# Turning the normalised mixer outputs of three heads in float32r, from copies, behind the next head's softmax

## The chip, the cores and the metric

The kernel runs as one program on one core of a Trainium2 chip. The metric is its device time in microseconds (us). The kernel before takes 1347.12 us, the median of three runs (1346.63 to 1347.56).

## What is computed

The reference is a two-layer backbone over 256 latent tokens and 256 context tokens of 1024 features. Layer 0 has an mLSTM mixer, layer 1 multi-head latent attention, and a gated ConvFFN follows each. Everything is float32. The change lies in the mLSTM mixer of layer 0. It has four heads with 512 value features each, and its output is:

```python
def out(h_in, s):
    Bq, T, _ = h_in.shape
    o = jax.nn.sigmoid(h_in @ w_og).reshape(Bq, T, M_HEADS, M_DV)
    hsum = o * s.transpose(0, 2, 1, 3).astype(h_in.dtype)
    return _head_rms_norm(hsum, norm_g) @ w_out
```

Here `s` is the result of the scan, which the kernel computes for a head as one masked, weighted product P v over all 512 tokens. So a head's tokens are multiplied by a gate, divided by their root mean square over the head's 512 features, scaled by a gain for each feature, and then multiplied by `w_out`, whose contraction runs over the features.

## The kernel before

**Products in three passes.** A float32 product is made of float32r products: every operand is kept as a float32r tile that holds its rounded value and a second one that holds the rest, and `mm3` (L425 to L434) issues first times first, first times second, second times first. Weights come from HBM in tiles of 128 x 1024, are rounded on ScalarE (L345) and their rest is formed on VectorE (L368). A transpose is a product with an identity matrix; `post` uses the float32 identity `ident`.

**A mixer head.** `w_qk(h)` makes the head's q and k from the convolved input: eight weight tiles with 24 matmuls each. `s_mm(h)` forms the scores S. `head(h, S)` is the softmax-like part: it loads two rows of gate values (`aB`, L1045), adds masks (`Am`), takes exponentials (`W`, L1087), multiplies them with S, normalises the rows to P and turns P on TensorE (L1118). `v_load(h)` loads the head's values `vr` and gates `oh`. `av(h)` multiplies P with v and the result with the gate (L1178); the four tiles of 128 tokens x 512 features that it gives are `tt`.

**What the change touches.** `post(h, tt)` takes them: four Squares with sums (L1188), a square root (L1189), a reciprocal, four scalings in place (L1192), then a `yield`; then sixteen transposes of 128 x 128 (L1198) in four groups, each group written out with the gain as a pair of float32r tiles `hn` (L1205 on ScalarE, L1206 on VectorE). `outmm("mout", ...)` multiplies `hn[k]` with `w_out`, for k from 0 to 15, with four k for each head; 12 matmuls a k.

**What sets the order.** `head`, `post` and others are generators, kept in the list `k.bg`. `tick` advances the first of the list by one `yield`; a generator that has ended costs one tick to be taken off. `w_qk` ticks twice after each of its eight weight tiles, and the output projection twice after each k from 0 to 7 and once after each k from 8 to 15. A planner then orders each engine's instructions: it follows the order in which the program issues them, takes something later where an instruction's inputs or its buffer are not there by its own estimate, and each engine runs its list in the order that results. The list of POOL holds the DMAs that are issued there: `vr`, `oh`, `aB`, the residual and gate rows.

**Before the change**, `post(h - 2)` stands ahead of `head(h - 1)` in the loop over heads for h = 2 and 3: norm at tick 1, transposes at tick 2, taken off at tick 3, the softmax at ticks 4 to 8 and P turned at tick 9. In the output projection `head(3)` stands first (ticks 1 to 6) and `post(2)` after it (ticks 8 and 9). `post(3)` runs behind k = 8 and 9 of the projection.

**Buffers.** Tiles of 128 x 512 float32 come from a pool called "s2" with NS = 15 buffers: `tt` (that is `oh`), S, `aB`, `Am`, `W`, `vr`, Squares' output `jk`. A tile of the pool can be written only when one of the 15 is free.

Of the kernel before, what the change touches and what calls it, by code (L numbers as in the profile page):

```python
# [7 lines left out]
F32 = mybir.dt.float32  # L8
F32R = mybir.dt.float32r
I32 = mybir.dt.int32  # L10
AF = mybir.ActivationFunctionType
ALU = mybir.AluOpType
# [21 lines left out]
NB, NRAW, NU, NS = 3, 3, 31, 15  # L34
# [366 lines left out]
class K:  # L401
# [73 lines left out]
    def setup(self):  # L475
        nc, p = self.nc, self.pool
        a = self.a
        self.sm = p.tile([128, a["sm"].shape[1]], F32, name="sm")
        self.sm0 = p.tile([128, NSM0], F32, name="sm0")
        jp = p.tile([128, 128], I32, tag="s2", name="jp", bufs=NS)  # L480
        nc.gpsimd.iota(jp, pattern=[[1, 128]], base=0, channel_multiplier=-1)
        self.jp = jp
        self.ident = p.tile([128, 128], F32, name="ident")
        self.mask = p.tile([128, 2, 128], F32, name="mask")
        self.k1 = p.tile([128, 1], F32, name="k1")
        nc.vector.memset(self.k1, 1.0)
        self.zero = p.tile([128, 512], F32R, tag="s2", name="zero", bufs=NS)
        nc.vector.memset(self.zero.bitcast(F32), 0.0)
        self.keps = p.tile([128, 1], F32, name="keps")
        nc.vector.memset(self.keps, EPS)  # L490
        self.cond = p.tile([128, 8, 32], F32, tag="s2", name="cond", bufs=NS)
        nc.gpsimd.memset(self.cond, 0.0)
        self.mod0 = p.tile([128, 2, 8, 2], F32, name="mod0")
        self.modc = {(0, c): self.mod0[:, c] for c in range(2)}
        self.gd = {}
        self.adav = p.tile([128, 32], F32, name="adav")
        nc.vector.memset(self.adav, 0.0)
        for l in range(2):
            for c in (3, 4) if l == 0 else (0, 1, 3, 4):
                self.modc[l, c] = p.tile([128, 8, 2], F32, name="mod%d%d" % (l, c))  # L500
            for c in (2, 5):
                self.gd[l, c] = self.dr.tile([2, D], F32, name="gd%d%d" % (l, c))
# [102 lines left out]
    def start_up(self):  # L605
# [47 lines left out]
        with self.tc.manual_schedule(engines={e.PE, e.DVE, e.Activation}):  # L653
            for _ in range(WARM):
                nc.tensor.matmul(idle, self.zero[:, 0:128], self.zero, start=True, stop=True)
            for step in STEPS:
                op, n = step[0], [int(x) for x in step[1:]]
                g = n[0]
                if op == "Q":
                    nc.scalar.activation(self.cond[:, :, 0:2], self.smc("cond").rearrange("p (a b) -> p a b", b=2),  # L660
                                         AF.Silu)
                    nc.vector.tensor_scalar(self.ident, self.jp, 0.0, None, op0=ALU.is_equal)
                    b1 = self.smc("ada_b")[:, 8:16]
                    nc.vector.tensor_scalar(b1, b1, 1.0, None, op0=ALU.add)
                elif op == "M":
                    nc.vector.tensor_scalar(self.mask[:, 0], self.jp, 0.0, NEG, op0=ALU.is_gt, op1=ALU.mult)
                    nc.vector.tensor_scalar(self.mask[:, 1], self.jp, 0.0, NEG, op0=ALU.is_lt, op1=ALU.mult)
                    self.jp = None
                elif op == "I":
                    for _ in range(g):  # L670
                        nc.tensor.matmul(idle, self.zero[:, 0:128], self.zero, start=True, stop=True)
                elif op in "Aab":
                    if g not in rows:
                        rows[g] = self.ps("adar")
                    self.ada_mm(rows[g], [(x, raw["a%d%d" % (g, x)]) for x in {"A": (0, 1), "a": (0,), "b": (1,)}[op]])
                elif op == "C":
                    adas[g] = self.ada_copy(rows[g])
                elif op == "T":
                    self.ada_T(rows[g], adas[g])
                elif op == "O":  # L680
                    self.ada_cols(g, rows[g])
                elif op == "E":
                    self.mod_tile(g)
                elif op == "H":
                    h = hT[g] = self.u("hT")
                    self.split(h[:, 0, :], h[:, 1, :], self.xT[g])
                elif op == "e":
                    h = hT[g] = self.u("hT")
                    x, (c, l) = self.xT[g], (slice(0, 256), slice(256, 512))
                    sh, sc = self.modc[0, 0][:, g], self.modc[0, 1][:, g]  # L690
                    nc.vector.tensor_scalar(x[:, c], x[:, c], sc[:, 1:2], sh[:, 1:2], op0=ALU.mult, op1=ALU.add)
                    nc.scalar.activation(h[:, 0, l], x[:, l], AF.Identity, bias=sh[:, 0:1], scale=sc[:, 0:1])
                    nc.vector.tensor_copy(h[:, 0, c], x[:, c])
                elif op == "l":
                    nc.vector.tensor_scalar(x[:, l], x[:, l], sc[:, 0:1], sh[:, 0:1], op0=ALU.mult, op1=ALU.add)
                    nc.vector.tensor_sub(h[:, 1], x, h[:, 0])
                elif op in "WwvyzKkU":
                    if op == "U":
                        g = "u"
                        raw["wu"] = raw["u0"]  # L700
                    if g not in w:
                        w[g] = [self.pool.tile([128, CW], F32R, tag="u", name="w0", bufs=NU) for _ in range(2)]
                    c = slice(256, nw) if op in "yz" else slice(0, 256 if op in "wv" else 768 if op == "U" else nw if g < 2 else 512)
                    hi, lo, src = w[g][0][:, c], w[g][1][:, c], raw["w%s" % g][:, c]
                    if op == "w":
                        nc.vector.tensor_copy(hi, src)
                    elif op in "WyKU":
                        nc.scalar.copy(hi, src)
                    if op in "WvzkU":
                        nc.vector.tensor_sub(lo, src, hi)  # L710
                else:
                    k, m = n
                    if m not in ps:
                        ps[m] = self.ps("up")
                    wk, o = (w["u"], k - 2) if m == 4 and k > 1 else (w[k], m)
                    c = slice(o * 128, (o + 1) * 128)
                    for i, j in {"V": ((0, 0), (0, 1), (1, 0)), "P": ((0, 0),), "L": ((1, 0),), "R": ((0, 1),)}[op]:
                        nc.tensor.matmul(ps[m], wk[i][:, c], hT[k][:, j], start=made[m] == 0, stop=made[m] == 23)  # L718
                        made[m] += 1
# [460 lines left out]
        self.PT = self.vh = self.oh = None  # L1180
        return r

    def post(self, h, tt):
        nc = self.nc
        ss = self.tiny(4, "ss")
        jk = self.s2("jk")
        for t in range(4):
            nc.scalar.activation(jk, tt[t], AF.Square, accum_out=ss[:, t:t + 1])  # L1188
        nc.scalar.activation(ss, ss, AF.Sqrt, bias=self.keps, scale=1.0 / 512.0)  # L1189
        nc.vector.reciprocal(ss, ss)  # L1190
        for t in range(4):
            nc.vector.tensor_scalar(tt[t], tt[t], ss[:, t:t + 1], None, op0=ALU.mult)  # L1192
        yield
        g = self.smc("mng")
        for e in range(4):
            pt = self.ps("hnT")
            for t in (2, 0, 1, 3):
                q = nc.tensor.transpose(pt[:, t * 128:(t + 1) * 128], tt[t][:, e * 128:(e + 1) * 128], self.ident)  # L1198
                if e or t != 2:
                    self.behind(q, [lead])  # L1200
                else:
                    lead = q
            k = h * 4 + e
            u = self.u("hn")
            nc.scalar.activation(u[:, 0], pt, AF.Copy, scale=g[:, k:k + 1])  # L1205
            nc.vector.scalar_tensor_tensor(u[:, 1], pt, g[:, k:k + 1], u[:, 0], op0=ALU.mult, op1=ALU.subtract)  # L1206
            self.hn[k] = u
        yield


    def bcast(self, row, name):
        ts = []
# [969 lines left out]
def build(tc, off, a, out):  # L2182
    es = ExitStack()
    with es:
        k = K(tc, es, off, a)
        nc = k.nc
# [16 lines left out]
        for h in range(H0):  # L2203
# [1 line left out]
            if h == 0:  # L2205
                gens.append(k.gate_chain())
            if h >= 2:
                gens.append(k.post(h - 2, tt))
            if h >= 1:
                gens.append(k.head(h - 1, S))  # L2210
            k.bg = gens
            k.w_qk(h, 2, (lambda: k.v_load(h - 1)) if h >= 1 else None)
# [4 lines left out]
        k.xc = None  # L2217
        hn = lambda i: (k.hn[i][:, 0], k.hn[i][:, 1])
        pc = k.acc4()
        k.bg = [k.head(3, S, True), k.post(2, tt)]  # L2220
        vs = k.v_steps(3)
        for i in range(8):
            k.outmm("mout", range(i, i + 1), hn, pc, 0, 16, 2, n2=ADA_M)
            next(vs, None)
        k.drain()
        tt = k.av(3)
        k.bg = [k.post(3, tt)]
        k.outmm("mout", range(8, 12), hn, pc, 0, 16, 1, n2=ADA_M)
        k.drain()
        tokr = a["tok"].rearrange("(t p) d -> t p d", p=128)  # L2230
# [132 lines left out]
```

## Time and profile before

| What | Value |
|---|---|
| median of three runs | 1347.12 us |
| the profiled execution, span from first to last instruction | 1345.3 us, 1.8 us below the median |
| TensorE (PE) busy | 1334.9 us |
| weight loads of TensorE (PEld) busy | 1120.2 us |
| VectorE (DVE), ScalarE (ACT), GpSimd (POOL) busy | 1059.0, 711.7, 141.5 us |
| transposes of `post` | 64, in four batches of 16 that begin at 465.06, 524.25, 598.46 and 615.22 us |
| turning of P | four times 12; those after head 0 at 487.39, 546.57 and, in two parts, 584.96 and 594.80 us |

The span is what the profiler saw between the first and the last instruction. PEld runs beside PE, so the two are not added. A matmul's duration is longer than its share of the pipeline: matmuls start closer together than they last, and the distance between starts tells what one costs. In a row of the time line stand start, duration, engine, line, operation, written tile, read tiles, shape and count; in brackets stands the idle time of the engine before it and what ended it. In a row of groups the busy time and the mean duration in ns stand behind the bar. DMA-issuing rows of POOL show the issue; "us to landing" is the time until the data are there.

### The profile page before, as it was taken

Reading aid. Unit: us, or ns where it says so; the run is one execution under the profiler, and the core shown is the slowest. Engines: PE = TensorE matmul, PEld = TensorE weight load, DVE = VectorE, ACT = ScalarE, POOL = GpSimd, SP = SyncE. Lnnn points to the kernel's source line nnn. Section 1 sums busy time; section 2 is a strip of 40 time slices with the busy share of each in tenths; the row PEclk is TensorE's granted clock in tenths of the full one; section 3 lists DMA queues with packets and bytes.
Section 4 is the critical chain, followed back from the end, with each engine's and each line's share of the span. In section 5 each row is a group of like instructions: output and inputs, shape, how many; then the busy total and the mean of one; then the engine's idle time right before and its main releaser. Section 6 shows DMA issues by size and latency. Waiting matters only on the chain.

```text
span 1345.3 us, 18750 instructions
## 1 busy us (share of the span) xinstructions
PE 1334.9 (99%) x6659; PEld 1120.2 (83%) x6659; DVE 1059.0 (79%) x1745; ACT 711.7 (53%) x1252; POOL 141.5 (11%) x236
## 2 busy tenths in 40 slices
PE   9999999999999999999999999999999999999997
PEld 5777888888888888888898888888888998988886
DVE  4798656678688696897979977758899889898874
ACT  4765444445744546474644334333566767676660
POOL 0222000011101011020002011111000002000100
PEclk9999999999999999999999999999999999999999
DMA  9988848889686384776628989967866437376750
GB/s 364 330 277 279 281 163 248 233 272 307 235 281 230 102 255 149 228 292 222 215 86 261 328 260 286 282 181 184 300 223 194 157 104 219 127 212 189 263 189 32
DMA packets 99885, 304.02 MB, mean 226 GB/s; under 512 B 12312, under 2 KB 25112, under 8 KB 99712
## 3 DMA queue, kind: packets, MB, share of 16 engines
q1 hardware_dynamic: 62992, 218.65, 48.6%
q0 software_dynamic: 26000, 66.75, 17.9%
q10 hardware_dynamic: 10800, 17.44, 3.6%
q8 instruction: 52, 0.85, 0.3%
q14 instruction: 41, 0.34, 0.1%
HBM read 272.21 MB, written 42.12 MB: 234 GB/s over the span
## 4 chain that ended last, share of the span: by engine, by line
PE 97%; DMA 1%; DVE 1%; ACT 0%; issue 0%; SPq 0%; DVEq 0%; ACTq 0%
PE fin L1503 8%; PE tok L430 6%; PE tok L434 6%; PE tok L433 6%; PE fin L433 6%; PE fin L434 6%; PE y L433 6%; PE fin L430 6%; PE y L434 6%; PE y L430 6%; PE qk L430 4%; PE qk L433 4%; PE qk L434 4%; PE up L718 2%; PE up L430 2%; PE up L434 1%
## 5 line engine op out<-in xcount | busy, mean ns | idle before, releaser
L368 DVE TENSOR_TENSOR w<-raw,w 128x1024 fp32r<-128x1024 f32 (+2 forms) x286 | 343.2, 1203 | 131.9 <-ACT w L345 129.7
L345 ACT CAST w<-raw 128x1024 fp32r<-128x1024 f32 (+2 forms) x286 | 296.2, 1037 | 282.4 <-PE tok L434 77.8
L544 DVE SCALAR_TENSOR_TENSOR junk<-ar,bc 128x1024 f32<-128x1024 f32 x128 | 156.1, 1219 | 5.2 <-ACT bc L586 2.3
L433 PE MATMUL fin<-h,w 128*128 128x512 f32 (+1 forms) x370 | 139.6, 377 | 0.0
L430 PE MATMUL fin<-h,w 128*128 128x512 f32 (+1 forms) x370 | 139.5, 377 | 0.0
L434 PE MATMUL fin<-h,w 128*128 128x512 f32 (+1 forms) x370 | 139.3, 377 | 0.0
L1503 PE MATMUL fin<-h,w 128*128 128x512 f32 (+1 forms) x636 | 111.1, 337 | 0.0
L1503 PEld LDWEIGHTS fin<-h,w 128*128 128x128 f32 x636 | 97.6, 190 | 13.2
L430 PE MATMUL qk<-xc,w 128*128 128x512 f32 x256 | 100.2, 391 | 0.0
L434 PE MATMUL qk<-xc,w 128*128 128x512 f32 x256 | 99.8, 390 | 0.0
L433 PE MATMUL qk<-xc,w 128*128 128x512 f32 x256 | 99.6, 389 | 0.0
L433 PEld LDWEIGHTS fin<-h,w 128*128 128x128 f32 x370 | 69.6, 188 | 13.0
L430 PEld LDWEIGHTS fin<-h,w 128*128 128x128 f32 x370 | 69.6, 188 | 12.9
L434 PEld LDWEIGHTS fin<-h,w 128*128 128x128 f32 x370 | 69.6, 188 | 12.6
L434 PEld LDWEIGHTS qk<-xc,w 128*128 128x128 f32 x256 | 48.0, 188 | 10.1
L430 PEld LDWEIGHTS qk<-xc,w 128*128 128x128 f32 x256 | 48.1, 188 | 9.8
L433 PEld LDWEIGHTS qk<-xc,w 128*128 128x128 f32 x256 | 48.1, 188 | 9.8
L430 PE MATMUL tok<-w,hT 128*128 128x512 f32 x128 | 49.9, 390 | 0.0
L433 PE MATMUL tok<-w,hT 128*128 128x512 f32 x128 | 49.8, 389 | 0.0
L434 PE MATMUL tok<-w,hT 128*128 128x512 f32 x128 | 49.8, 389 | 0.0
L735 ACT ACTIVATE fg<-fg 128x512 f32<-128x512 f32 (+1 forms) x44 | 23.1, 525 | 50.0 <-DVE fg L733 43.9
L368 DVE TENSOR_TENSOR wu<-raw,wu 128x1024 fp32r<-128x1024 f32 (+1 forms) x37 | 43.8, 1203 | 3.5 <-ACT wu L345 3.2
(486 smaller groups left out, 3125.7 us busy)
## 6 DMA issues: line engine op xcount, KB each, us to landing
raw<-in_ws SPq DMA_DIRECT2D x282, 512.0 KB, 4.5
ar<-in_adaT SPq DMA_DIRECT2D x80, 512.0 KB, 6.0
t4d<-in_ws POOLq DMA_DIRECT2D x20, 512.0 KB, 9.1
adaw<-in_ada SPq DMA_DIRECT2D x16, 512.0 KB, 8.0
zr<-fd ACTq DMA_DIRECT2D x33, 128.0 KB, 4.6
xmd<-xr POOLq DMA_DIRECT2D x16, 256.0 KB, 4.4
xcd<-cv POOLq DMA_DIRECT2D x16, 256.0 KB, 4.9
xs<-xmd POOLq DMA_DIRECT2D x16, 256.0 KB, 6.0
```

Source lines behind the costliest of these rows:

```text
L345: self.cast = k.nc.scalar.copy(h[:, :cols], src)
L368: i = self.k.nc.vector.tensor_sub(l[:, :n], src, h[:, :n])
L430: q = mm(out, w[0], x[0], start=start, stop=False, skip_group_check=on)
L433: mm(out, w[0], x[1], start=False, stop=False, skip_group_check=on)
L434: mm(out, w[1], x[0], start=False, stop=stop, skip_group_check=on)
L544: nc.vector.scalar_tensor_tensor(o, w, 1.0, self.bc[j], op0=ALU.mult, op1=ALU.mult, accum_out=col[:, k, j:j + 1])
L718: nc.tensor.matmul(ps[m], wk[i][:, c], hT[k][:, j], start=made[m] == 0, stop=made[m] == 23)
L735: nc.scalar.activation(tmp[:, :n], tmp[:, :n], AF.Silu)
L1503: self.nc.tensor.matmul(ps[:, 0:256] if x else ps, w[x][:, k * 128:(k + 1) * 128], h[:, 0:256] if x else h, start=i == 0 and not k0, stop= ...
```

## The change

Three things change in the mixer of layer 0.

- For heads 0, 1 and 2, each scaled tile `tt[t]` is copied by a DMA on POOL's queue, word for word, into a tile `rr` of the type float32r from the pool "s2". The transposes read `rr` and a float32r identity `identr`, and write PSUM as float32r. For head 3 they read `tt` and the float32 identity as before.
- A new generator `around` issues the norm and the copies of `post` in its first tick, then all of the next head's `head`, and then the rest of `post`. In the loop over heads the softmax so comes at ticks 2 to 6, P is turned at tick 7 and the transposes of `post` are issued at tick 9. In the output projection the norm of head 2 moves ahead of `head(3)`.
- `post` has one `yield` more between norm and transposes. For head 3 the transposes so come behind k = 10 of the projection and not k = 9.

`identr` is written once, on VectorE, beside the masks at the end of the start-up.

```diff
+        self.identr = p.tile([128, 128], F32R, name="identr")
...
+                    nc.vector.tensor_scalar(self.identr, self.jp, 0.0, None, op0=ALU.is_equal)
...
-    def post(self, h, tt):
+    def post(self, h, tt, copy=True):
...
+        rr = []
         for t in range(4):
             nc.vector.tensor_scalar(tt[t], tt[t], ss[:, t:t + 1], None, op0=ALU.mult)
+            if copy:
+                r = self.pool.tile([128, 512], F32R, tag="s2", name="rr", bufs=NS)
+                nc.gpsimd.dma_start(r.bitcast(F32), tt[t])
+                rr.append(r)
+        src, ident, dt = (rr, self.identr, F32R) if copy else (tt, self.ident, F32)
+        yield
         yield
...
-                q = nc.tensor.transpose(pt[:, t * 128:(t + 1) * 128], tt[t][:, e * 128:(e + 1) * 128], self.ident)
+                q = nc.tensor.transpose(pt[:, t * 128:(t + 1) * 128].bitcast(dt), src[t][:, e * 128:(e + 1) * 128], ident)
...
+    def around(self, post, head):
+        next(post)
+        yield
+        yield from head
+        yield from post
...
             if h >= 2:
-                gens.append(k.post(h - 2, tt))
-            if h >= 1:
+                gens.append(k.around(k.post(h - 2, tt), k.head(h - 1, S)))
+            elif h >= 1:
                 gens.append(k.head(h - 1, S))
...
-        k.bg = [k.head(3, S, True), k.post(2, tt)]
+        k.bg = [k.around(k.post(2, tt), k.head(3, S, True))]
...
-        k.bg = [k.post(3, tt)]
+        k.bg = [k.post(3, tt, False)]
```

## The prediction

> **What bounds the kernel now.** I read the page first, then the groups of TensorE by shape, then the time lines around the places that the change touches.
>
> ```profile
> PE 1334.9 (99%) x6659; PEld 1120.2 (83%) x6659; DVE 1059.0 (79%) x1745; ACT 711.7 (53%) x1252; POOL 141.5 (11%) x236
> PE 97%; DMA 1%; DVE 1%; ACT 0%; issue 0%; SPq 0%; DVEq 0%; ACTq 0%
> ```
>
> TensorE (PE) is busy for 1334.9 of 1345.3 us, and 97% of the chain of waits is its own work. So a copy, a scale or a DMA is worth something only if PE waits for it, and a gain must come out of PE's own time. The change touches 48 transposes of PE, in three batches of 16. What a batch costs is read from the time line of PE around each (start, duration, count):
>
> ```profile
> 462.73 0.39 PE L434 MATMUL qk<-xc,w 128*128 128x512 f32 x1
> ...
> 464.77 0.39 PE L434 MATMUL qk<-xc,w 128*128 128x512 f32 x1
> 465.06 2.03 PE L1198 MATMUL hnT<-ident,oh 128*128 128x128 f32 x16
> 466.85 0.48 PE L430 MATMUL qk<-xc,w 128*128 128x512 f32 x1
> 467.17 0.40 PE L433 MATMUL qk<-xc,w 128*128 128x512 f32 x1
> ...
> 523.96 0.39 PE L434 MATMUL qk<-xc,w 128*128 128x512 f32 x1
> 524.25 2.03 PE L1198 MATMUL hnT<-ident,oh 128*128 128x128 f32 x16
> 526.04 0.48 PE L430 MATMUL qk<-xc,w 128*128 128x512 f32 x1
> 526.35 0.40 PE L433 MATMUL qk<-xc,w 128*128 128x512 f32 x1
> ...
> 598.23 0.39 PE L434 MATMUL y<-w,hn 128*128 128x512 f32 x1
> 598.46 1.91 PE L1198 MATMUL hnT<-ident,oh 128*128 128x128 f32 x16
> 600.12 0.47 PE L430 MATMUL y<-w,hn 128*128 128x512 f32 x1
> 600.44 0.39 PE L433 MATMUL y<-w,hn 128*128 128x512 f32 x1
> ```
>
> Nine undisturbed 512-column matmuls lie between 462.73 and 464.77: 0.227 us a step. From the last matmul before a batch to the second after it lie 2.40, 2.39 and 2.21 us; less two normal steps (0.45), the batches cost 1.94, 1.94 and 1.75 us, 5.63 in all. The third is undisturbed: 1.75 / 16 = 0.109 us per transpose. The first two hold about 0.18 more each, since their scaled inputs arrive while they run.
>
> **What a float32r transpose costs.** The trace has none, nor any float32r matmul under 256 columns; two things can limit it, the streaming of the moving identity and the load of the stationary block.
>
> ```profile
> L433 PE MATMUL qk<-xc,w 128*128 128x512 f32 x256 | 99.6, 389 | 0.0
> L1503 PE MATMUL fin<-h,w 128*128 128x256 f32 x320 | 44.6, 282 | 0.0
> L764 PE MATMUL gates<-cv,gw 128*32 128x512 f32 x32 | 3.8, 598 | 0.0
> L1198 PE MATMUL hnT<-ident,oh x64: 270/273/328, 465.1 to 616.9; 128*128 128x128 f32 x64
> L718 PE MATMUL up<-hT,w x120: 387/389/504, 10.1 to 48.0; 128*128 128x512 f32 x120
> 1149.72 2.32 PE L1346 MATMUL y<-wu,oT 128*128 128x256 f32 x18
> 1151.88 1.36 PE L1439 MATMUL fin<-h,wu 128*128 128x256 f32 x10
> ```
>
> Streaming: the first two rows are float32r tiles (every product of L430 to L434 and L1503 is). 256 columns more cost 107 ns, so 128 columns stream in 53.5. The gate matmuls (third row) read plain float32, and 512 columns take 209 ns longer than in float32r: one more pass. A float32r matmul of 128 columns would by this last 282 - 53.5 = 229; the present transposes last 273, 44 more, so they too run two passes, and 0.109 us is two times 53.5 and little else. In float32r I expect one.
>
> Load: a matmul that had to wait for its own load shows it in its duration. For the transposes the longest less the median is 328 - 273 = 55 ns, for float32r matmuls (L718) 504 - 389 = 115. Which holds for a float32r transpose, no row says. If what is loaded is decided by the transpose, 55 hides behind the stream; if by the type, 115 is the step.
>
> So the step p has these ends: 55 from below (load and stream overlapped, nothing on top), 120 from above (what 18 float32r matmuls of 256 columns take each, 2.16 / 18). I take 62: one pass of 53.5 plus some of the 13 ns that a 512-column step of 227 has beyond its 214 of streaming. It is the nearer value because plain float32 in the same transpose already loads in 55.
>
> A rule of the Trainium skill speaks against it. "TensorE: Matmul & The Clock Gate", section "LDWEIGHTS (loading the stationary operand)", puts a load at its number of columns divided by 1.2, in ns, whatever the rows: an estimate by that page of 107 for these blocks, and then nothing is gained. The 115 of L718 agrees with it, the 55 of the present transposes does not, so here the rule holds for one kind of load and is open for the new one.
>
> **The change, part by part.**
>
> Transposes: a batch now costs 15 p, and its last one hides only a part of the 115 ns load of the float32r matmul behind it: 15 x 0.062 + 0.115 = 1.05 us. The inputs will long be there, so the 0.18 of the first two batches goes too. Saved: 0.89 + 0.89 + 0.70 = 2.5 us. With p = 55: 0.94 a batch, 2.8 saved. With p = 120: 1.92 a batch, 0.02 + 0.02 - 0.17, or 0.1 lost.
>
> Copies: twelve DMAs of 256 KB on POOL's queue, four behind each normalisation.
>
> ```profile
> oh<-od POOLq DMA_DIRECT2D x16, 256.0 KB, 4.2
> 467.18 1.65 POOL L1133 DMA_DIRECT2D vr<-vd  x3 [43.37 <-PE hnT L1198]
> L1118 PE MATMUL PT<-ident,W x12: 271/272/273, 487.4 to 488.6; 128*128 128x128 f32 x12
> L444 ACT CAST v<-vr x4: 621/622/622, 494.8 to 496.4; 128x512 fp32r<-128x512 f32 x4
> 505.05 0.39 PE L430 MATMUL av<-v,PT 128*128 128x512 f32 x1
> ```
>
> Issuing four takes 4 x 0.54 and the last lands about 4.2 later: 6.4 us. They are issued at the first step of the background work and read at the ninth, four weight tiles later: 96 x 0.227 = 21.8 us in the q/k projection, with 24 matmuls a tile, and 10.9 in the output projection, with 12. So PE doesn't wait; uncovered, it would cost up to 6.4 per batch. Queued behind them on POOL are the next v and gate tiles (vr, oh) and aB. They need buffers of the pool "s2", which the copies keep until the moved batch, now some 20 us later; the vr loads, which today start at 467.2 when the transposes free their buffers, can start only when the turning of P (today at 487.4, then one tile earlier) and the moved batch free some, at about 482 to 487. Eight issues and the landing bring the last v in by about 494, and v is cast today at 494.8 to 496.4 for a product at 505.05. Cost nothing.
>
> Softmax of the next head: two steps, one weight tile (5.4 us), earlier. Its end sets PE's slot for turning P, and the planner places that by its own estimate; I allow 0.2 us of PE waits for the two slots.
>
> Third place, the output projection: here the norm of head 2 stood behind the softmax of head 3 and now stands ahead of it, on ACT above all.
>
> ```profile
> 577.26 0.40 ACT L1087 ACTIVATE W<-aB,gcol 128x128 f32<-128x128 f32 x1
> 579.49 1.05 ACT L345 CAST w<-raw 128x1024 fp32r<-128x1024 f32 x1 [1.83 <-PE y L434]
> 588.59 0.63 ACT L1188 ACTIVATE jk<-oh 128x512 f32<-128x512 f32 x1
> 589.12 0.19 ACT L1188 ACTIVATION_READ_ACCUMULATOR jk<-oh 128x1 f32 x1
> 591.59 1.28 ACT L1189 ACT_TABLE_LOAD   x1
> 592.89 0.30 ACT L1189 ACTIVATE ss<-ss,keps 128x4 f32<-128x4 f32 x1
> 593.91 0.74 DVE L1105 SCALAR_TENSOR_TENSOR W<-W,R 128x512 f32<-128x512 f32 x1
> 594.80 1.06 PE L1118 MATMUL PT<-ident,W 128*128 128x128 f32 x8
> ```
>
> Squares 4 x 0.82, table 1.28, root 0.30, and the table for Exp must come back, 1.28: 6.1 us ahead of the exponentials, of which the idle 1.83 before 579.49 takes a part, so the softmax ends up to 4.3 us later. The last P is ready at 594.65 and turned at 594.80, so there is no slack in that slot; but its eight turns end at 594.80 + 8 x 0.109 = 595.7, and up to the batch at 598.46 stand 12 matmuls, 2.8 us of PE work that the planner can put in front. I allow 0.2.
>
> The last head's batch has no copy but comes one step later, past 12 matmuls.
>
> ```profile
> 617.63 2.72 DVE L1206 SCALAR_TENSOR_TENSOR hn<-hnT,sm,hn 128x512 fp32r<-128x512 f32 x4
> L666 DVE TENSOR_SCALAR mask<-jp x1: 221/221/221, 42.2 to 42.2; 128x128 f32<-128x128 int32 x1
> ```
>
> The last of all transposes starts at 616.9 (row L1198), so its batch began at 616.9 - 15 x 0.109 = 615.3. Four writes of the second halves take the 2.72 from 617.63 on, so the first is done by 618.3: 3.0 us after the batch began. Moved, only 1.75 of transposes and one tile (2.7) lie between: covered by 1.4 us, and a shortfall beyond that would be lost. ACT reloads the root's table once more there, 1.28, within the tile by which the batch is later. The identity in float32r is one more DVE instruction of 0.22 us beside the mask at 42.2, with DVE work for PE not due at once; uncovered, 0.22.
>
> Sum: -2.5 + 0.4 = -2.1 us. The profiled execution spans 1345.3, 1.8 below the median of 1347.12; carried over, 1343.2 and 1345.0 us.
>
> **Rivals.**
> 1. The load sets the step (or two passes remain): p = 109 to 120, saved 0.4 at best (the waits of the first two batches), and 0.5 lost with the allowance: 1346.7 to 1347.6, take 1347.1. For it the 115 of every float32r load; against it the 55. It is also the case that the change doesn't do what its type says. By the section of the Trainium skill named above it is the one that comes true.
> 2. Slower: PE waits for head 3's P. Place: the eight turns that stand at 594.80. If the written order keeps them before the 12 matmuls and the 6.1 us of ACT work are all in front, PE stands 6.1 us: -2.5 + 6.1 = +3.6, 1350.7. With 4.3 it is +1.8. It decides from 2.5 us of waiting on, and passes 0.2% from 5.2. For it the 0.15 us of slack; against it the spare 2.8 us of matmuls.
> 3. Narrow float32r is slow: as much as plain float32, which the trace issues twice (x32 for 16 gate products) with two passes each, 4 x 53.5 = 214. 48 x 0.214 - 5.63 = +4.6: 1351.7. No row speaks for it except that nothing narrower than 256 is used.
> 4. The best end: p = 55, no wait anywhere: 1344.3.
>
> **How the numbers follow.** 0.2% is 2.7 us, about what a measurement of this kernel tells from no change. Forecast 0.48, own range 1344.3 to 1346.3; its lower edge and the fourth rival carry 0.13 past 2.7 us. Rival 1 0.25, all within. Rival 2 0.18, of it 0.12 past +2.7. Rival 3 0.05. Left, 0.04, half each, for orders that shift far behind. Faster 0.13 + 0.02 = 0.15; slower 0.12 + 0.05 + 0.02 = 0.19; same 0.66. The range goes from 1344.1 to 1350.5: below lies 0.06, above rivals 2 and 3 in part, 0.13.
>
> **What would show it.** The hnT row of TensorE: a duration near 229 and batches of about 1.05 us; a duration near 273 and 1.75 us is rival 1. Loads of hnT at a mean of 140 ns mean the short kind, 188 the long (the float32r rows). The idle column and long durations of PT by L1118 show rival 2, as do matmuls between the softmax's end and that slot. vr landing after 500 would prove the buffers wrong, and a PE row waiting on a copy the cover. Over 1348 us without such a wait, I have missed a cost.

## The result, and the profile after

The changed kernel takes 1384.9 us (median of five runs, 1380.96 to 1385.89) against 1347.12: a ratio of 1.0275, 95% interval 1.0262 to 1.0287. It is 37.8 us slower, where 1345.0 was predicted and 1350.5 was the upper end.

The page of the kernel after has, for the engines' busy time and for the chain of waits:

```profile
PE 1343.7 (97%) x6659; PEld 1127.1 (81%) x6659; DVE 1060.5 (77%) x1746; ACT 715.3 (52%) x1254; POOL 148.4 (11%) x248
PE 89%; issue 6%; DVE 2%; DMA 2%; POOL 1%; ACT 0%; DVEq 0%; SPq 0%; POOLq 0%
```

The span is 1383.1 us, 37.8 more than before. TensorE (PE) is busy 8.8 us longer for the same 6659 instructions, so it stands idle 29.0 us more. Both have to be explained. The view of what PE's matmuls waited for, between 400 and 660 us (in all, times, longest), names one place for nearly all of the added idle time:

```profile
PE PT L1120 <- DVE W L1107: 28.8, 6, 9.1
```

L1120 is the turning of P (L1118 before the change), L1107 the last step of the softmax on VectorE (DVE). The six waits are two in each of the three heads whose softmax now stands behind a norm. PE's time line shows those of head 1, and what comes after them:

```profile
480.09 0.39 PE L434 MATMUL qk<-xc,w 128*128 128x512 f32 x1
482.23 0.66 PE L1120 MATMUL PT<-ident,W 128*128 128x128 f32 x4 [1.76 <-DVE W L1107]
492.02 1.97 PE L1120 MATMUL PT<-ident,W 128*128 128x128 f32 x8 [9.12 <-DVE W L1107]
493.64 0.78 PE L430 MATMUL qk<-xc,w 128*128 128x512 f32 x1
494.21 0.63 PE L433 MATMUL qk<-xc,w 128*128 128x512 f32 x1
494.64 0.63 PE L434 MATMUL qk<-xc,w 128*128 128x512 f32 x1
...
497.05 0.39 PE L434 MATMUL qk<-xc,w 128*128 128x512 f32 x1
497.28 0.39 PE L430 MATMUL qk<-xc,w 128*128 128x512 f32 x1
```

PE comes to the turning at 480.5 and stands 1.8 and 9.1 us. Afterwards a matmul takes 0.43 us from start to start (494.21 to 494.64) instead of 0.23 (497.05 to 497.28). The busy time of each engine by stretch tells why (the stretch and its length, then PE, PEld, DVE, ACT, POOL, then the granted TensorE clock, the DMA share and GB/s):

```profile
455.00:480.00 25.00, 25.00 (x116) 20.85 (x115) 9.79 (x21) 13.24 (x28) 4.38 (x8) 1.00 0.45 148
482.60:492.00 9.40, 0.29 (x3) 0.05 (x1) 9.37 (x24) 2.69 (x8) 3.18 (x6) 0.53 0.91 313
492.00:496.00 4.00, 3.98 (x14) 3.50 (x15) 3.91 (x7) 1.66 (x3) 0.00 (x0) 0.50 0.77 294
```

The clock granted to TensorE falls to half while it stands, and stays there for nearly 5 us of work. That accounts for the 8.8 us: PE is "busy" longer because it runs slower. By the same view four stretches, behind the waits of all three heads, hold 20.6 us of PE's work at half clock; as an estimate, half of it, 10.3 us, is added time, less the 1.3 us by which the transposes are shorter. The Trainium skill, "TensorE: Matmul & The Clock Gate", section "Part 1: The HAM clock gate (the "warmup" mystery)", says that an idle array is put to half its rate; the 0.50 agrees.

Upstream, the time line of GpSimd (POOL), whose list holds the DMAs issued there, after the change and then before it:

```profile
465.15 2.32 POOL L1198 DMA_DIRECT2D rr<-oh  x4 [53.79 <-DVE oh L1195]
467.46 1.08 POOL L1047 DMA_DIRECT2D aB<-ad  x2
468.51 1.01 POOL L1678 DMA_DIRECT2D t4d<-in_ws  x2
480.66 0.58 POOL L1135 DMA_DIRECT2D vr<-vd  x1 [11.13 <-DVE R L1096]
...
482.89 1.06 POOL L1135 DMA_DIRECT2D vr<-vd  x2 [0.32 <-issue]
```

```profile
418.19 0.54 POOL L1045 DMA_DIRECT2D aB<-ad  x1 [7.19 <-DVE junk L544]
422.28 0.54 POOL L1045 DMA_DIRECT2D aB<-ad  x1 [3.55 <-PE PT L1118]
```

Before, POOL issued aB for head 1 at 418 to 422, some 45 us ahead of the exponentials that use it. Now the four copies stand in front of it in POOL's list and wait 53.79 us for the scaling of `oh`; aB can only follow at 467.46. The first exponential on ScalarE (ACT) of that head, after and then before:

```profile
476.03 0.62 ACT L1089 ACTIVATE W<-aB,gcol 128x384 f32<-128x384 f32 x1 [3.56 <-DMA aB<-ad]
```

```profile
464.79 0.40 ACT L1087 ACTIVATE W<-Am,gcol 128x128 f32<-128x128 f32 x1
```

It starts 11.2 us later, while the place of turning P has moved 7 us earlier (487.39 before, reached at 480.5 now). ACT's wait for aB is 3.56 us of the 11.2. The rest is its place in ACT's list, which the load of the exponential's table just ahead of it shows, after and then before:

```profile
471.19 1.28 ACT L1089 ACT_TABLE_LOAD   x1
```

```profile
463.50 1.28 ACT L1087 ACT_TABLE_LOAD   x1
```

The transposes of the change itself, in the view of the tile and in PE's time line (a weight load stands as PEld):

```profile
L1207 PEld LDWEIGHTS hnT<-identr,rr x48: 137/142/230, 500.5 to 639.3; 128*128 128x128 f32 x48
L1207 PE MATMUL hnT<-identr,rr x48: 221/252/455, 500.7 to 639.4; 128*128 128x128 f32 x48
```

```profile
500.71 1.48 PE L1207 MATMUL hnT<-identr,rr 128*128 128x128 f32 x16
502.02 0.46 PE L430 MATMUL qk<-xc,w 128*128 128x512 f32 x1
```

Sixteen take 502.02 - 500.71 = 1.31 us, 0.082 each. PE waits for no copy in front of them.

### The profile page after: what moved, and what is told of

Its sections match the earlier page's. It is cut to its first block, busy times and chain, and to the rows that moved or that the text cites. A ratio compares the mean times of both kernels' runs of the same rounds, so it can differ in the third digit from the quotient of the medians.

```text
span 1383.1 us, 18800 instructions
## 1 busy us (share of the span) xinstructions
PE 1343.7 (97%) x6659; PEld 1127.1 (81%) x6659; DVE 1060.5 (77%) x1746; ACT 715.3 (52%) x1254; POOL 148.4 (11%) x248
## 4 chain that ended last, share of the span: by engine, by line
PE 89%; issue 6%; DVE 2%; DMA 2%; POOL 1%; ACT 0%; DVEq 0%; SPq 0%; POOLq 0%
PE fin L1519 8%; PE y L433 6%; PE y L430 6%; PE tok L430 6%; PE y L434 6%; PE tok L434 6%; PE tok L433 6%; PE fin L433 6%; PE fin L434 6%; PE fin L430 6%; PE qk L430 3%; PE qk L433 3%; PE qk L434 3%; PE up L720 2%; DMA aB<-ad 2%
## 5 line engine op out<-in xcount | busy, mean ns | idle before, releaser
L430 PE MATMUL qk<-xc,w 128*128 128x512 f32 x256 | 101.7, 397 | 0.0
L433 PE MATMUL qk<-xc,w 128*128 128x512 f32 x256 | 100.8, 394 | 0.0
L434 PE MATMUL qk<-xc,w 128*128 128x512 f32 x256 | 100.7, 393 | 0.0
L434 PEld LDWEIGHTS qk<-xc,w 128*128 128x128 f32 x256 | 48.8, 191 | 10.3
```

Source lines behind the costliest of these rows:

```text
L430: q = mm(out, w[0], x[0], start=start, stop=False, skip_group_check=on)
L433: mm(out, w[0], x[1], start=False, stop=False, skip_group_check=on)
L434: mm(out, w[1], x[0], start=False, stop=stop, skip_group_check=on)
```

## The experiments

Three theories can each make P late. **Q**: aB stands behind the copies in POOL's list. **B**: the copies take "s2" buffers that the softmax needs. **O**: the turning of P simply stands one weight tile too early in PE's order, copies or none. The medians (the kernel before was 1347.05, 1347.33 and 1347.21 in the three sets of runs):

| Kernel | us | ratio to before, 95% |
|---|---|---|
| the change, rows of a first | 1372.46 | 1.0188 (1.0174 to 1.0202) |
| the order alone | 1355.23 | 1.0067 (1.0055 to 1.008) |
| the type alone | 1346.36 | 0.9995 (0.9987 to 1.0004) |
| copies and type in the old order | 1362.76 | 1.0121 (1.0107 to 1.0135) |
| rows of a first, copies in other buffers | 1361.84 | 1.0111 (1.0096 to 1.0126) |
| rows of a first, P later | 1357.77 | 1.0074 (1.0057 to 1.0091) |
| all three | 1355.91 | 1.0064 (1.0049 to 1.0079) |
| the order alone, P later | 1347.2 | 1.0 (0.9991 to 1.001) |
| all three, old output projection | 1345.87 | 0.9991 (0.9981 to 1.0) |
| the change, copies on ScalarE's queue | 1367.83 | 1.015 (1.0137 to 1.0164) |

**Rows of a first.** The change, with aB issued one step ahead of the norm and the copies ("a" stands for aB).

```diff
     def around(self, post, head):
+        next(head)
+        yield
         next(post)
```

> The changed kernel, but the next head's loads of aB (and its masks) are issued one step ahead of the norm and the copies, so that on POOL's list aB stands before rr; transposes, copies, buffers and the place of the turning of P stay. Theory Q (aB waits on POOL's queue behind the copies, which wait for the scaled head): aB is loaded some 45 us before it is used, as before the change, the PE waits at P vanish with the half clock behind them, 1345 to 1349 us. Theory O (the softmax and the turning of P stand too early in PE's order): no help, 1375 to 1385. Theory B (the copies take four of the 15 buffers and the softmax waits for buffers): no help, 1375 to 1385.

1372.46: 12.4 us come back, so aB's place is a cause, and not the only one. Most of it comes back in the output projection, where PE's waits for P fall from 7.9 to 1.6 us. Behind head 0's norm PE still stands at the second part of the turning, though what the exponentials waited for is no longer aB (PE's time line, ACT's waits between 455 and 495 us, ACT's time line):

```profile
490.07 1.97 PE L1120 MATMUL PT<-ident,W 128*128 128x128 f32 x8 [9.08 <-DVE W L1107]
```

```profile
ACT W L1089 <- DMA rr<-oh: 2.1, 2, 1.6
```

```profile
471.25 1.28 ACT L1089 ACT_TABLE_LOAD   x1
```

W waits for the copies: it gets buffers that `oh` leaves, and `oh` is left only when its copy has landed. The waits themselves are 2.1 us; beside them the exponentials still stand as late in ACT's list as in the change, although aB was issued at 418.50.

**The order alone.** The change without copies, float32 transposes throughout.

```diff
-    def post(self, h, tt, copy=True):
+    def post(self, h, tt, copy=False):
```

> The changed kernel without copies: post reads the scaled tiles and the float32 identity for all heads, but norm, next softmax and transposes stand in the new order. Theory Q: nothing stands on POOL in front of aB, 1346 to 1350 us. Theory O: as slow as the changed kernel, 1370 to 1385. Theory B: 1346 to 1350, since no buffer more is taken.

1355.23, between the theories: the order costs 8.2 us by itself. PE's time line, and the last step of the softmax on DVE:

```profile
480.50 0.60 PE L1120 MATMUL PT<-ident,W 128*128 128x128 f32 x4
484.00 1.23 PE L1120 MATMUL PT<-ident,W 128*128 128x128 f32 x8 [2.90 <-DVE W L1107]
```

```profile
483.11 0.74 DVE L1107 SCALAR_TENSOR_TENSOR W<-W,R 128x512 f32<-128x512 f32 x1
```

P is complete at 483.85; PE is there at 481. Before the change it came at 487.39. Head 2's turning has a wait of the same length; the view of PE's waits shows none in the output projection.

**The type alone.** The order of before; the scaling writes a float32r tile, no DMA. The scaled values are thereby rounded to float32r, which the change doesn't do.

```diff
...
-            nc.vector.tensor_scalar(tt[t], tt[t], ss[:, t:t + 1], None, op0=ALU.mult)
+            r = self.pool.tile([128, 512], F32R, tag="s2", name="rr", bufs=NS) if h < 3 else tt[t]
+            nc.vector.tensor_scalar(r, tt[t], ss[:, t:t + 1], None, op0=ALU.mult)
+            tt[t] = r
...
```

The lines left out make `identr` and hand it to the transposes.

> The kernel before with its order, without DMA copies: for heads 0 to 2 the scaling writes a float32r tile, which rounds the values (the second part of a product's operand then lacks what the rounding took away, so less is computed exactly), and the transposes run in float32r. It is the price of the type alone. With the step of 0.082 us that the changed kernel shows for its first batch, a batch is 15 x 0.082 + 0.115 = 1.35 us beside 1.75 undisturbed: 0.4 saved in each of three, 1.2 us, 1345.9 us (1345.3 to 1346.8). If the step is 0.062 as I forecast, 2.1 saved, 1345.0.

1346.36, 0.7 below before, not to be told from no change. The type can bring little more: 48 steps shorter by 0.109 - 0.082 us are 1.3.

**Copies and type in the old order.**

```diff
-                gens.append(k.around(k.post(h - 2, tt), k.head(h - 1, S)))
-            elif h >= 1:
+                gens.append(k.post(h - 2, tt))
+            if h >= 1:
```

and the same in the output projection, with one `yield` between norm and transposes.

> The changed kernel's copies and float32r transposes in the order of before: norm, copies, transposes, then the softmax. Theory Q: in the loop over heads the copies still stand before aB on POOL, so aB comes as late as in the changed kernel, but P is turned one weight tile (5.4 us) later; PE waits some 4 to 6 us less at P in two places, and 5 to 8 us in each of two for the copies; nothing in the output projection, where aB is ahead: 1358 to 1372 us. Theory O: only the waits for the copies, 1350 to 1358. Theory B: as the changed kernel, 1375 to 1385.

1362.76. Here PE waits for the copies, and nowhere for P:

```profile
470.72 1.05 PE L1206 MATMUL hnT<-identr,rr 128*128 128x128 f32 x8 [2.06 <-DMA rr<-oh]
472.86 1.26 PE L1206 MATMUL hnT<-identr,rr 128*128 128x128 f32 x8 [1.08 <-DMA rr<-oh]
```

So the change's later place of the transposes does spare PE these waits. The time lies in the range of theory Q, but without the waits for P on which that range rests: aB is late here too (issued at 467.21), and the turning stands at 492.88, late enough.

**Copies in other buffers.** Rows of a first, and the copies in the pool "u", whose tiles hold two of them each.

```diff
-                r = self.pool.tile([128, 512], F32R, tag="s2", name="rr", bufs=NS)
+                if t % 2 == 0:
+                    two = self.u("rr")
+                r = two[:, t % 2]
```

> The kernel with the rows of a loaded ahead of the copies (1372.46), and the float32r copies no longer take four of the 15 s2 buffers but two of the u tiles. In that kernel's trace the exponentials of W waited for the copies' transfers (ScalarE on DMA rr<-oh: 2.1 us behind head 0's norm, 3.2 behind head 1's), because W gets the buffers that the normed outputs leave only when a copy has landed. Theory B (buffers): the exponentials start some 5 to 7 us earlier, the two 9 us waits of TensorE for P shrink to the 3 us that the kernel with the order alone had, and the time is 1353 to 1359. Theory O (the place of the turning alone, the buffers harmless): 1369 to 1373, the 9 us waits stay.

1361.84: 10.6 us less. ACT waits for no copy any more, the table of the exponential is loaded earlier, and head 1's long wait is that of the order alone (ACT's time line, then PE's):

```profile
466.67 1.28 ACT L1089 ACT_TABLE_LOAD   x1
```

```profile
482.56 1.94 PE L1120 MATMUL PT<-ident,W 128*128 128x128 f32 x8 [2.75 <-DVE W L1107]
```

B is a cause. The time is 3 us above its range, because PE now waits 0.8 and 6.8 us in the output projection; "All three" shows where that comes from.

**P later.** Rows of a first, copies in "s2", and two more ticks ahead of the turning of P of heads 1 and 2.

```diff
             yield
         yield
+        if h in (1, 2):
+            yield
+            yield
         self.PT = []
```

> The kernel with the rows of a loaded ahead of the copies (1372.46), the copies in s2 as there, and the turning of P of heads 1 and 2 is put two ticks later in TensorE's order, behind 120 of the next head's matmuls as before the change instead of behind 96. Those 24 matmuls are 24 x 0.227 = 5.4 us of cover. Theory O (the cost is that TensorE comes to the turning too early): the two waits of 9.2 and 9.3 us shrink to about 4 each, and with them the stretch at half clock: 1355 to 1364. If the softmax slips along with its place (its work is put into VectorE's order by the same plan), the waits stay: 1369 to 1373.

1357.77. The waits for P of heads 1 and 2 are one each, the longest of 3.6 us instead of 9.1: the softmax doesn't slip along with the place. In the output projection PE waits 1.7 us for P.

**All three.** Both edits, with rows of a first.

> Both: the copies in u tiles and the turning of P of heads 1 and 2 two ticks later, with the rows of a loaded ahead of the copies. Left of the change are the copies themselves, the float32r turning and its later place. If POOL's order, the buffers and the place of the turning of P are all there is, nothing waits any more and the time is that of before less what float32r saves (0.7 us in the kernel with the type alone) plus at most the small waits of the output projection: 1345.5 to 1349. If the copies cost something else (transfers that crowd out weights, more work for the engines), 1352 or more.

1355.91, so something was left. PE waits for P only in the output projection now, 0.8 and 6.8 us. POOL's time line there, and ACT's wait for these loads (ACT's waits from 570 to 606 us):

```profile
586.85 2.23 POOL L1203 DMA_DIRECT2D rr<-oh  x4 [40.04 <-DVE oh L1198]
589.07 2.13 POOL L1155 DMA_DIRECT2D vr<-vd  x4
```

```profile
ACT v L444 <- DMA vr<-vd: 4.2, 2, 3.6
```

The values of head 3 (vr, last issued at 577.6 before the change) stand behind the copies of head 2, and a cast of v stands ahead of most of head 3's exponentials in ACT's list, so P waits too. It is what Q describes, with another victim. But this wait came in with the edit of the copies' tiles: the kernel with P later, which differs from this one only in having the copies in "s2", issues all of head 3's vr ahead of the copies.

```profile
576.33 1.07 POOL L1155 DMA_DIRECT2D vr<-vd  x2 [25.88 <-PE av L434]
577.39 1.06 POOL L1047 DMA_DIRECT2D aB<-ad  x2
584.19 1.06 POOL L1155 DMA_DIRECT2D vr<-vd  x2 [5.74 <-DVE wu L368]
597.87 2.20 POOL L1201 DMA_DIRECT2D rr<-oh  x4 [12.61 <-DVE oh L1198]
```

Head 3's vr takes its tiles from "u" as well, as the kernel's `v_steps` has it; that this is why the planner put it behind the copies is likely, but not shown.

**All three, and the old output projection.** The norm of head 2 stands behind the softmax of head 3 again, and head 2 has no copies.

```diff
-        k.bg = [k.around(k.post(2, tt), k.head(3, S, True))]
+        k.bg = [k.head(3, S, True), k.post(2, tt, False)]
```

> The kernel with rows of a first, copies of heads 0 and 1 in u tiles and the turning of P two ticks later (1355.91 us), and in the output projection the order and the float32 turning of head 2 of before, so that its two waits for head 3's P (1.0 us at 597.34 and 7.1 us at 598.96) have no cause left. If the three causes (POOL's order, buffers, the place of the turning of P) are all of the 37.8 us, what is left are the copies of two heads behind the softmax and 32 float32r transposes at 0.082 instead of 0.109 us, 0.9 us less: 1345.9 to 1347.4, 1346.4 as the likeliest. If the copies cost anything by themselves: 1348 or more.

1345.87. PE waits for P nowhere, and with copies and float32r turning for heads 0 and 1 left in, the 37.8 us are gone. It is 1.3 us below before; the interval ends at 1.0, so that isn't to be told from no change.

**The order alone, P later.** The check on O without copies.

> The kernel with the order alone (no copies, float32 turning; 1355.23), with the turning of P of heads 1 and 2 put back behind 120 matmuls. Theory O: its two waits of 3.06 us in the turning of P (at 480.83 and 544.49 us) are covered by 5.4 us more work, and the time returns to that of before: 1346.5 to 1348.5. Rival (the 8 us are from the norm's place and the shifted transfers, not from the turning's): 1352 to 1356.

1347.2: the whole 8.2 us were the place of the turning.

**Copies on ScalarE's queue.** The change, with one word exchanged.

```diff
-                nc.gpsimd.dma_start(r.bitcast(F32), tt[t])
+                nc.scalar.dma_start(r.bitcast(F32), tt[t])
```

> The changed kernel (1384.9) with one edit: the copies are issued from ScalarE's queue instead of POOL's, all orders and buffers as in the change. Theory Q (what cost 12.4 us is that aB is queued behind the copies on POOL, which wait for the norm): aB lands before the first exponential needs it as when it is put ahead by hand, and the time falls to 1366 to 1378. Rival (the copies' transfers themselves or their tick, whichever queue issues them): 1382 to 1388. Buffers and the place of the turning stay as in the change, so under no theory does it come below 1360.

1367.83: 17.1 us come back by the queue alone, so Q is shown. One wait for P is left in each of the three heads:

```profile
PE PT L1120 <- DVE W L1107: 15.4, 3, 6.0
```

They fit O and B, which this kernel keeps: the table of the exponential is loaded at 471.34 here, as late as with aB first by hand. No run separates the two on this queue.

By these steps the 37.8 us run: 12.4 (rows of a first), 10.6 (buffers), 5.9 (P later, heads 1 and 2), 10.0 (output projection), and 1.3 below before. The shares hold in this order of undoing only, since late aB, late buffers and an early place lengthen the same wait: O is worth 8.2 alone, and Q 17.1 by the other queue. The 10.6 are also too little for the buffers, and the 10.0 too much for the output projection, since the move to "u" brought in a wait there that the last step took out. Putting aB ahead by hand gave less than the other queue, probably as it also moved the norm a step back: the fourth Square stands at 465.21 there, at 461.69 with the order alone (ACT's time lines).

## Why the prediction was wrong

**Transposes, -2.5 us.** The direction was right. The loads stayed the short kind (median 142 ns; the forecast named a mean near 140), and rival 1, a step of 0.109 or more, didn't come true. The Trainium skill ("TensorE: Matmul & The Clock Gate", section "LDWEIGHTS (loading the stationary operand)") has a load take its columns divided by 1.2, by an estimate 107 ns here; the measured step of 82 ns, load included, is shorter. But the step is 0.082, not 0.062: 20 ns on 48 is 1.0 us of the 2.5. The median duration of 252 ns, forecast near 229, says the same.

**"So PE doesn't wait" for the copies.** Right. In the old order they cost 16.4 us over the type alone (1362.76 - 1346.36); at the ninth tick nothing waits.

**Copies, "Cost nothing".** This step failed. It named aB as queued behind the copies, and then worked out a due time for vr alone. For head 1 that one was met: all four vr were issued by 483.95 and landed at most 4.7 us later, against the 494.8 of the forecast. But aB had the nearer due time, the first exponential at 464.79, and the row that would have told it, POOL issuing aB at 418 to 422, is not in the sum. On another queue the same copies cost 17.1 us less. What counted was not the 6.4 us that the copies take, but that they wait in an in-order list for the norm, 53.79 us, and that everything behind waits with them.

**Buffers.** Here too the effect was named and only vr priced. The softmax's own W takes buffers from the same 15, and its due time comes first. Other tiles for the copies gave 10.6 us. The sign that I set for this error, vr landing after 500, couldn't have shown it.

**Softmax one tile earlier, allowance 0.2.** Failed: 8.2 us in the kernel with the order alone. The planner's estimate was trusted to place the turning where P is ready, but the order put it at 481 and P was ready at 483.85. The row for the right sum was in the trace of before: P's last step, 484.79 + 0.74 there, ended 1.9 us ahead of the turning at 487.39. The turning moved 6.9 us earlier (487.39 to 480.50: one weight tile, and the batch of transposes that no longer stands in front), so the softmax had to end 5.0 us earlier. It ended 1.7 earlier (its last step starts at 483.11 against 484.79). Two ticks later the turning cost nothing (1347.2).

**Output projection, allowance 0.2, and rival 2.** The place was right, PE waits at both parts of head 3's turning:

```profile
624.06 1.11 PE L1120 MATMUL PT<-ident,W 128*128 128x128 f32 x4 [3.25 <-DVE W L1107]
635.60 1.94 PE L1120 MATMUL PT<-ident,W 128*128 128x128 f32 x8 [4.69 <-DVE W L1107]
```

Its mechanism was not. When the copies are absent, the norm ahead of the softmax on ACT costs PE no wait in the output projection that its view of waits shows; with them the last aB of all, for head 3, is issued at 612.6 us, and at 547.9 before (the views of the tile aB, first and last issue, after and before):

```profile
L1047 POOL DMA_DIRECT2D aB<-ad x8: 536/550/577, 368.3 to 612.6; - x8
```

```profile
L1045 POOL DMA_DIRECT2D aB<-ad x8: 536/536/577, 368.0 to 547.9; - x8
```

**What stood nowhere in the sum:** the half clock behind the waits, which makes the 8.8 us by which PE is busy longer. The last head's batch and the float32r identity, put at nothing, cost nothing that the traces show.

## What to carry to other kernels

A DMA that waits for late data holds up every DMA behind it in its engine's list, as aB here; so when one is put into a list, write down the issue time and first use of each that follows it, not only of the one that comes to mind. An experiment that moves tiles to another pool can make a wait of its own there; compare its traces with those of the kernel before that step. When a step is moved earlier, its slack before (here 1.9 us) has to be set against the distance it moves. And a wait of TensorE is dearer than its length, since the clock may drop behind it.

## What the runs showed of the hardware

**The clock falls after short waits too, but not always.** With the order alone PE stood twice, 2.9 us each. Behind the first the granted clock of the next 4 us is 0.60; behind the second no matmul is slower, and the stretch around it stands at 1.00:

```profile
484.00:488.00 4.00, 4.00 (x15) 3.34 (x16) 4.00 (x6) 1.66 (x3) 0.00 (x0) 0.60 0.79 255
544.00:552.00 8.00, 5.10 (x30) 4.19 (x29) 7.97 (x13) 3.18 (x6) 0.54 (x1) 1.00 0.81 287
```

Section "Part 1: The HAM clock gate (the "warmup" mystery)" of the Trainium skill's "TensorE: Matmul & The Clock Gate" explains this with a window of about 3.4 us that runs freely; two waits of one length with two outcomes agree with it, and no run here was made to test it. The clock's records in the packed traces agree too: a stretch at half clock between two at the full one lasts 3.41, 6.83, 10.24 or 13.65 us, whole multiples of 3.41, in every run that has one.

**A float32r transpose of 128 x 128 costs 0.082 us a step**, between one streaming pass (53.5 ns) and the two of float32 (0.109 us), with loads as short as in float32. What the 28 ns above one pass are, the runs leave open.
